# A decoder layer on one core: x ahead of w_ada, a new division of the start, and modulation loads spread

## The chip, the core and the metric

The kernel runs on one core of a Trainium2 chip. The metric is the device time of one execution, in microseconds (us), lower being better. A core has TensorE (PE: matmuls and transposes), VectorE (DVE), ScalarE (ACT), GpSimd (POOL) and SyncE (SP, which here issues nearly all transfers); each works through its own instructions in order, and semaphores make one wait for another.

## The reference, cut to what matters

One layer for 256 tokens of width 2048, all in float32. A vector `c` gives shift, scale and gate; the normed and modulated x goes through one input projection of 9296 columns; two kinds of attention, eight heads each, follow, and an output projection.

```
def _hybrid_layer(x, c, w_ada, b_ada, g_norm, w_in, ...):
    mod = jax.nn.silu(c) @ w_ada + b_ada
    shift, scale, gate = jnp.split(mod, 3, axis=-1)
    h = _rms_norm(x, g_norm) * (1.0 + scale[:, None, :]) + shift[:, None, :]
    proj = h @ w_in
    ...
    y = jnp.concatenate([ya, yb], axis=-1) @ w_out
    return x + gate[:, None, :] * y
```

`w_ada` is 2048 x 6144 (50 MB), `w_in` 2048 x 9296 (76 MB), `w_out` 2048 x 2048 (17 MB). All of the weights are read once.

## The kernel before, in words

**Matmuls.** Contraction runs over 16 k-tiles of 128 rows. `h` is kept transposed (k-tile by 256 tokens). Each float32 product is made of three matmuls in the fp32r type: a weight tile is cast to a high part `wh` (ScalarE, `cast_hi`, L306) and the rest `wl` (VectorE, `cast_lo`, L316), `h` likewise to `hhi` and `hlo`, and hi x hi, lo x hi and hi x lo are summed in PSUM (L760 to L762). For 512 columns, one k-tile and the two token tiles that is six matmuls. Column groups are named by what they hold (z, q, k, v, or the indexer's i0 to i2) and by a quad: `b0`, `b1`, `a0`, `a1`, so `qb0` is 512 columns of q.

**Passes.** The modulation of a k-tile needs two loads of `w_ada`, one for its shift and one for its scale, 128 columns by all 2048 rows each (1 MB, `gemv`, L273: a multiply and sum on VectorE against `s_row`, which holds silu(c)). It is made in chunks: k-tile 0, then 1, then two at a time. So the input projection goes over its column groups in passes, each taking the k-tiles whose modulation is known by then. The results of a pass leave PSUM in `evac`: the first of a group is copied (ScalarE, L662), later ones are added to it (VectorE, L664). A first pass with one k-tile takes a quad's four groups from one load (kind `quad`).

**What sets the order.** `loads` is a list written ahead by a planner that counts in `n_kt`, units of one k-tile by 512 columns: modulation loads come into it by `ADA_AT`, `ADA_FIRST` and `ADA_GAP`, in `between`. `issue` sends them from SyncE in this order into four `raw` buffers of 1 MB; a load waits until the buffer of the fourth load ahead of it has been cast or summed. `in_order` keeps a block's instructions in written order on each engine; elsewhere the framework's scheduler places them.

**The start.** The first part of `w_ada`, then x in eight tiles (token tile t, 512 columns j), then two halves of the second `w_ada` load with the first weights between them. ScalarE squares the x tiles (L339); VectorE (L342) and GpSimd (`rsqrt`, L135, L136) make `rx`, 1/rms of each token; x is scaled by it (L350, one tile on GpSimd, L348), transposed on TensorE into PSUM (`ptx`, L360) and copied out, times `g_norm`, as `xnT` (`x_gain`, L365). `build_h` makes `h` of a chunk from `xnT` and the modulation `mmod`. The transposes of later k-tiles and their copies stand among the matmuls of the first quads.

Of the kernel before, what the change touches and what calls it, by code (L numbers as in the profile page):

```python
# [35 lines left out]
# The modulation is made in chunks of k-tiles, shift and scale together; the input projection goes over its  # L36
# column groups in passes, each taking the k-tiles whose modulation is known by then.
# [12 lines left out]
def hybrid_block(ctx: ExitStack, tc: tile.TileContext, x, cols, w_ada_t, w_in, w_out, out):  # L50
# [24 lines left out]
    def in_order():  # L75
        # queues each of the block's instructions behind the one before it on its engine, over all such blocks
# [16 lines left out]
    # distance table: query tile 0 against keys 0..127, query tile 1 against keys 0..255  # L93
# [15 lines left out]
    # s = silu(c), and the products of the head gains with -1/sqrt(HD)  # L109
# [34 lines left out]
    # a load of w_ada: 128 of its columns, over all rows; h0, h1 bound the part of the rows  # L144
# [38 lines left out]
    while turn:  # L183
        while ready and (ready[0][0] <= n_kt or known == pos[turn[0]]):
# [38 lines left out]
    # the first weights come before the last part of the first chunk of the modulation  # L223
    n_start = 2 * CHUNKS[0][1] + 1
    loads.insert(n_start - 1, loads.pop(n_start))
    n_issued = 0
    late = []

    def issue(upto):
        nonlocal n_issued  # L230
        while n_issued < min(upto, len(loads)):
            ld = loads[n_issued]
            raw = rawp.tile([P, 2048], F32, tag="raw", name=f"raw{n_issued}")
            if ld["kind"] == "ada":
                h0, h1 = ld["h"]
                ld["v"] = raw[:, :h1 - h0]
                nc.sync.dma_start(ld["v"], w_ada_t[ld["col"] * P:(ld["col"] + 1) * P, h0:h1])
                while late:
                    nc.sync.dma_start(*late.pop(0))
            elif ld["kind"] == "quad":  # L240
                # the column groups of a quad are 1024 apart
# [562 lines left out]
```

## Time and profile before

| what | value |
|---|---|
| time, median of 3 runs | 578.87 us (578.55 to 581.14) |
| span of the profiled execution | 577.5 us |
| median of the runs over that span | 1.4 us |
| TensorE busy | 550.7 us, 95% |
| VectorE busy | 443.4 us, 77% |
| ScalarE busy | 325.4 us, 56% |
| GpSimd busy | 49.3 us, 9% |
| moved by DMA | 150.08 MB, 260 GB/s on average |

The profile shows one execution; its own time is not told apart from its span, so the median of the runs stands beside it. Busy shares are averages over stages with different limits: the first 50 us (x, the first modulation, two quads), the passes of the input projection until about 250 us, a stretch in which attention runs beside the last pass, and the output projection. In rows of the timeline a line is the start, the duration, the engine, the source line, the operation, what is written and read, and in brackets the idle time before it with what ended it. Neighbouring instructions of an engine overlap by about 0.1 us in such rows, so the step from start to start is the cost of one among many.

### The profile page before, as it was taken

To read this page: it belongs to the slowest core of one execution; us is meant where nothing else is said; L and a number is where in the kernel's file an instruction comes from. 1 tells how busy PE (TensorE), PEld (TensorE's weight loads), DVE (VectorE), ACT (ScalarE), POOL (GpSimd) and SP (SyncE) were. 2 spreads that over 40 slices of the span, in tenths; PEclk is the share of its full clock that TensorE was granted. 3 is DMA by queue.
4 is the path that set the end of the run, shared out by engine and by line. 5 is a ranking of instruction groups with operands and counts; after the bars stand their busy time and mean duration, and the time that the engine had idled before them with its cause. 6 is when DMAs were issued, how large, how long until landed. Compare 5 with 4: busy or idle time off the path is not lost.

```text
span 577.5 us, 7394 instructions
## 1 busy us (share of the span) xinstructions
PE 550.7 (95%) x2626; PEld 457.4 (79%) x2626; DVE 443.4 (77%) x675; ACT 325.4 (56%) x667; POOL 49.3 (9%) x61
## 2 busy tenths in 40 slices
PE   2869999999999999998999999999999999999996
PEld 2548888888878998976768888888877888887885
DVE  4876879898899797888979995788668576458452
ACT  5898563434435353567655567555766785554340
POOL 4100000000000000102101012010330210000000
PEclk8789999999999999999999999999999999999999
DMA  8988988989998898887864476777556468445701
GB/s 290 370 298 316 396 330 305 337 322 345 351 346 273 338 344 315 306 312 268 297 236 159 150 276 239 247 281 273 212 182 219 146 228 282 145 150 190 245 36 36
DMA packets 59669, 150.08 MB, mean 260 GB/s; under 512 B 3056, under 2 KB 9456, under 8 KB 53616
## 3 DMA queue, kind: packets, MB, share of 16 engines
q1 hardware_dynamic: 58480, 147.51, 71.4%
q10 hardware_dynamic: 1152, 2.10, 1.2%
q8 instruction: 20, 0.33, 0.2%
q14 instruction: 17, 0.14, 0.1%
HBM read 147.50 MB, written 2.10 MB: 259 GB/s over the span
## 4 chain that ended last, share of the span: by engine, by line
PE 80%; ACT 8%; DVE 4%; DMA 3%; POOL 2%; issue 2%; SPq 0%; DVEq 0%; ACTq 0%; POOLq 0%
PE mm_y_o L760 5%; PE mm_y_o L761 5%; PE mm_y_o L762 5%; PE mm_h_qa L760 2%; PE mm_h_ka L761 2%; PE mm_h_qa L762 2%; PE mm_h_qa L761 2%; PE mm_h_ka L762 2%; PE mm_h_ka L760 2%; PE mm_h_za L761 2%; PE mm_h_i L760 2%; PE mm_h_zb L762 2%; PE mm_h_zb L761 2%; PE mm_h_qb L760 2%; PE mm_h_qb L761 2%; PE mm_h_qb L762 2%
## 5 line engine op out<-in xcount | busy, mean ns | idle before, releaser
L306 ACT ACTIVATE wh<-raw 128x1024 fp32r<-128x1024 f32 (+3 forms) x192 | 187.1, 993 | 158.2 <-DMA raw<-in_w_in 60.6
L316 DVE TENSOR_TENSOR wl<-raw,wh 128x1024 fp32r<-128x1024 f32 (+3 forms) x192 | 215.2, 1140 | 61.9 <-ACT wh L306 61.4
L273 DVE CUSTOM_DVE_ANT_0 raw<-raw,s_row 128x2048 f32<-128x2048 f32 (+1 forms) x49 | 110.6, 2257 | 13.9 <-DMA raw<-in_w_ada_t 13.8
L760 PE MATMUL mm_y_o<-wh,yT 128*128 128x512 f32 x128 | 51.7, 404 | 0.0
L761 PE MATMUL mm_y_o<-wl,yT 128*128 128x512 f32 x128 | 49.9, 390 | 0.0
L762 PE MATMUL mm_y_o<-wh,yT 128*128 128x512 f32 x128 | 49.8, 390 | 0.0
L760 PE MATMUL mm_h_i<-wh,hhi 128*128 128x384 f32 (+1 forms) x96 | 31.5, 333 | 0.5 <-DVE p_i L664 0.5
L762 PE MATMUL mm_h_i<-wh,hlo 128*128 128x384 f32 (+1 forms) x96 | 31.5, 329 | 0.0
L761 PE MATMUL mm_h_i<-wl,hhi 128*128 128x384 f32 (+1 forms) x96 | 31.5, 328 | 0.0
L760 PE MATMUL mm_h_za<-wh,hhi 128*128 128x512 f32 x64 | 26.3, 413 | 4.6 <-ACT wh L306 4.6
L762 PEld LDWEIGHTS mm_y_o<-wh,yT 128*128 128x128 f32 x128 | 24.0, 188 | 5.3 <-DVE yT L554 0.2
L760 PEld LDWEIGHTS mm_y_o<-wh,yT 128*128 128x128 f32 x128 | 24.1, 188 | 4.8 <-ACT yT L553 0.2
L761 PEld LDWEIGHTS mm_y_o<-wl,yT 128*128 128x128 f32 x128 | 24.1, 188 | 4.6
L760 PE MATMUL mm_h_kb<-wh,hhi 128*128 128x512 f32 x64 | 26.0, 406 | 0.2 <-ACT p_zb L662 0.2
L760 PE MATMUL mm_h_vb<-wh,hhi 128*128 128x512 f32 x64 | 25.7, 403 | 0.2 <-ACT p_qb L662 0.2
L760 PE MATMUL mm_h_zb<-wh,hhi 128*128 128x512 f32 x64 | 25.9, 408 | 0.0
L761 PE MATMUL mm_h_za<-wl,hhi 128*128 128x512 f32 x64 | 25.7, 402 | 0.1
L760 PE MATMUL mm_h_qb<-wh,hhi 128*128 128x512 f32 x64 | 25.7, 401 | 0.0
L760 PE MATMUL mm_h_qa<-wh,hhi 128*128 128x512 f32 x64 | 25.7, 409 | 0.0
L760 PE MATMUL mm_h_ka<-wh,hhi 128*128 128x512 f32 x64 | 25.4, 402 | 0.0
L762 PE MATMUL mm_h_za<-wh,hlo 128*128 128x512 f32 x64 | 25.3, 398 | 0.0
L760 PE MATMUL mm_h_va<-wh,hhi 128*128 128x512 f32 x64 | 25.2, 397 | 0.0
(215 smaller groups left out, 1208.4 us busy)
## 6 DMA issues: line engine op xcount, KB each, us to landing
raw<-in_w_in SPq DMA_DIRECT2D x51, 1024.0 KB, 6.0
raw<-in_w_ada_t SPq DMA_DIRECT2D x47, 1024.0 KB, 6.7
raw<-in_w_out SPq DMA_DIRECT2D x16, 1024.0 KB, 5.1
raw<-in_w_in SPq DMA_DIRECT2D x17, 512.0 KB, 4.5
raw<-in_w_in SPq DMA_DIRECT2D x11, 768.0 KB, 6.2
x<-in_x SPq DMA_DIRECT2D x8, 256.0 KB, 6.9
xr<-in_x ACTq DMA_DIRECT2D x8, 256.0 KB, 6.5
raw<-in_w_in SPq DMA_DIRECT2D x3, 672.0 KB, 5.5
```

The lines of the kernel that those rows point to most:

```text
L273: nc.vector.tensor_tensor_reduce(out=ld["v"], in0=ld["v"], in1=s_row[:, h0:h1], scale=1.0, scalar=0.0, op0=ALU.mult, op1=ALU.add, accum_ou ...
L306: nc.scalar.activation(hi[:, :n, :w], v, AF.Copy)
L316: nc.vector.tensor_tensor(lo[:, :n, :w], v, sb["hi"][:, :n, :w].bitcast(F32), op=ALU.subtract)
L760: nc.tensor.matmul(ps, a_hi, sb["hi"][:, i, :w], start=st, stop=False)
L761: nc.tensor.matmul(ps, a_hi, sb["lo"][:, i, :w], start=False, stop=False)
L762: nc.tensor.matmul(ps, a_lo, sb["hi"][:, i, :w], start=False, stop=en)
```

## The change

What it does, in the order of the program:

- x's eight tiles are issued first; then the two first `w_ada` loads, whole, in five pieces (1024, 1024 | 1024, 512, 512 rows), each piece with a sum of its own (`PARTS`); then the first quad's `q` group, its other three groups, and the second quad. Until then the second quad stood behind four loads of modulations.
- The loads of modulations that follow come at `ADA_NEXT`, then each 5.5 units as before.
- The eight squares are made by ScalarE (six) and VectorE (two); of the scales by `rx`, five are on ScalarE and three on GpSimd. All 32 transposes of x stand ahead of the first matmul. The result for k=8 to 15 is copied to SBUF; k=0 too; k=1 to 7 stay in PSUM until `build_h` reads them there.
- `g_norm` is no longer multiplied into `xnT`, but into the modulation's scale (`build_h`, and `start_mod` on GpSimd for k-tile 0).
- A quad's groups are cast two at a time, in the order q, k, v, z (for the first quad q alone, k with v, z alone); of a quad's evacuations, those of the second token tile of a pair's second group are on VectorE.
- `build_gate` waits for two steps between its addition and its transposes.

```diff
-ADA_AT, ADA_FIRST, ADA_GAP, ADA_LAG, GATE_AT, GATE_GAP = 4, 4, 5.5, 2, 150, 8
+ADA_NEXT, ADA_GAP, ADA_LAG, GATE_AT, GATE_GAP = (8, 8, 11, 14, 17, 20), 5.5, 2, 150, 8
+PARTS = ((0, 1024, 2048), (0, 1024, 1536, 2048))
...
+    for ld, parts in zip(loads, PARTS):
+        ld["parts"] = list(zip(parts, parts[1:]))
...
+    ada_at = list(ADA_NEXT)
+    ada_at += [ADA_NEXT[-1] + ADA_GAP * (i + 1) for i in range(len(ada) - len(ada_at))]
...
-        if ada and n_kt >= ada_at:
-            for _ in range(ADA_FIRST if ada_at == ADA_AT else 1):
-                ld = ada.pop(0)
...
+        if ada and n_kt >= ada_at[0]:
+            ada_at.pop(0)
+            ld = ada.pop(0)
+            loads.append(ld)
+            if "end" in ld:
+                ready.append((n_kt + (ADA_LAG if ld["end"] > 1 else 0), CHUNKS[ld["end"]][1]))
...
+            first = len(loads) == len(PARTS)
+            for lo, hi in ((0, 1), (1, 3), (3, 4)) if first else ((0, 2), (2, 4)):
+                for i in range(lo, hi):
+                    members[i]["pair"] = (lo, hi)
...
+            if (kind, c, o) == ("mod", 0, 3):
+                start_mod()
...
+        sb["i"] = ld.get("i", 0)
+        if sb["i"]:
+            sb["hi"] = subs[j - 1]["hi"]
+            return
...
     def start_mod():
...
-        nc.vector.tensor_tensor(ss[:, :m], ss[:, :m], bmod[:, :m], op=ALU.add)
+        nc.gpsimd.tensor_scalar(ss[:, 5:6], ss[:, 0:1], ss[:, 1:2], bmod[:, 0:1], op0=ALU.add, op1=ALU.add)
+        nc.gpsimd.tensor_scalar(ss[:, 6:7], ss[:, 2:3], ss[:, 3:4], bmod[:, 1:2], op0=ALU.add, op1=ALU.add)
+        nc.gpsimd.tensor_scalar(ss[:, 6:7], ss[:, 6:7], gcol[:, 0:1], 0.0, op0=ALU.mult, op1=ALU.add)
...
         if b == 0:
...
+            nc.vector.scalar_tensor_tensor(ss[:, 6:7], ss[:, 4:5], gcol[:, 0:1], ss[:, 6:7],
+                                           op0=ALU.mult, op1=ALU.add)
+            ss = ss[:, 5:7]
+            cast_lo(0)
         else:
             nc.vector.tensor_tensor(ss[:, :2 * n], ss[:, :2 * n], bmod[:, 2 * k0:2 * k1], op=ALU.add)
+            nc.vector.tensor_tensor(ss[:, n:2 * n], ss[:, n:2 * n], gcol[:, k0:k1], op=ALU.mult)
...
+            src = xnT[k]
+            if 0 < k < 8:
+                src, xnT[k] = ptx[k // 2][:, k % 2 * L:(k % 2 + 1) * L], h_tile(f"xnT{k}")
...
+    with in_order():
+        for i in range(6):
+            x_square(i, "act")
+            if i == 3:
+                x_rsqrt(0)
+        for i in range(6, 8):
+            x_square(i, "dve")
+        x_rsqrt(1)
+        for t, j, eng in ((0, 0, "act"), (0, 2, "act"), (0, 1, "pool"), (0, 3, "act"),
+                          (1, 0, "act"), (1, 2, "pool"), (1, 3, "act"), (1, 1, "pool")):
+            x_scale(t, j, eng)
+        for t in range(2):
+            for j in (0, 2, 3, 1):
+                x_transpose(t, j)
+        for k in (0, 8, 9, 10, 11):
+            x_copy(k)
+    with in_order():
+        for i in range(n_start):
+            gemv(loads[i])
+        next_load = n_start
+        cast_hi(0)
+        for _ in build_h(0):
+            pass
+        for k in range(12, 16):
+            x_copy(k)
...
+                    if "pair" in ld and t == 1 and ld["i"] == 1:
+                        nc.vector.tensor_copy(proj[g, t][:, :w], ps[:, :w])
```

What stands in the program's order, at three places. The first is the start of SyncE's transfers, behind `cc`. Before:

```order
L237 DMA raw_148<-in_w_ada_t 128x2048
L331 DMA x_0_150<-in_x 128x512
...
L331 DMA x_3_164<-in_x 128x512
L237 DMA raw_171<-in_w_ada_t 128x1024
L249 DMA raw_173<-in_w_in 128x512
L237 DMA raw_175<-in_w_ada_t 128x1024
L239 DMA raw_173<-in_w_in 128x3x512
L237 DMA raw_209<-in_w_ada_t 128x2048
L237 DMA raw_212<-in_w_ada_t 128x2048
L237 DMA raw_214<-in_w_ada_t 128x2048
L237 DMA raw_315<-in_w_ada_t 128x2048
L253 DMA raw_317<-in_w_in 128x4x512
```

and now (of x's eight tiles the first and the last stand here, in both):

```order
L342 DMA x_0_148<-in_x 128x512
...
L342 DMA x_3_162<-in_x 128x512
L244 DMA raw_164<-in_w_ada_t 128x1024 x2
L244 DMA raw_167<-in_w_ada_t 128x1024
L244 DMA raw_167<-in_w_ada_t 128x512 x2
L252 DMA raw_171<-in_w_in 128x512
L252 DMA raw_171<-in_w_in 128x3x512
L252 DMA raw_268<-in_w_in 128x4x512
L244 DMA raw_270<-in_w_ada_t 128x2048
L244 DMA raw_272<-in_w_ada_t 128x2048
L260 DMA raw_325<-in_w_in 128x2x512
L260 DMA raw_383<-in_w_in 128x2x512
```

The second quad (`raw_317`, now `raw_268`) has moved from behind four loads of modulations to ahead of them, and only two come before the first weights of two k-tiles.

The second place is VectorE at the second quad. Before (`raw_315` is a load of modulations, `raw_317` the quad):

```order
L397 TENSOR_TENSOR hlo_351<-xnT_251,hhi_348 128x256
L273 ISA raw_315,mmod_328<-raw_315,s_row 128x2048
L273 ISA mmod_328 128x1
L316 TENSOR_TENSOR wl_333<-raw_317,wh_331 128x512
L316 TENSOR_TENSOR wl_366<-raw_317,wh_364 128x512
L316 TENSOR_TENSOR wl_393<-raw_317,wh_391 128x512
L316 TENSOR_TENSOR wl_409<-raw_317,wh_407 128x512
```

and now:

```order
L328 TENSOR_TENSOR wl_329<-raw_268,wh_327 128x1024
L680 COPY p_vb_1_341<-mm_h_vb_1_332 128x512
L274 ISA raw_270,mmod_389<-raw_270,s_row 128x2048
L274 ISA mmod_389 128x1
L328 TENSOR_TENSOR wl_357<-raw_268,wh_355 128x1024
L680 COPY p_ka_1_381<-mm_h_ka_1_372 128x512
L274 ISA raw_272,mmod_389<-raw_272,s_row 128x2048
```

The quad's four low parts are two, and a sum of a modulation load now stands between them.

The third place is TensorE behind the quads, where the first groups of two k-tiles begin. Before (`wh_425` is the only load's cast that it needs there):

```order
L760 MATMUL mm_h_za_0_468<-wh_425,hhi_242 128x512
L760 MATMUL mm_h_za_1_469<-wh_425,hhi_242 128x512
L761 MATMUL mm_h_za_0_468<-wl_427,hhi_242 128x512
L762 MATMUL mm_h_za_0_468<-wh_425,hlo_245 128x512
L760 MATMUL mm_h_za_0_468<-wh_425,hhi_348 128x512
```

and now (`wh_392` is cast from `raw_325`, `wh_418` from `raw_383`):

```order
L775 MATMUL mm_h_za_0_444<-wh_392,hhi_279 128x512
L775 MATMUL mm_h_za_1_445<-wh_392,hhi_279 128x512
L775 MATMUL mm_h_qa_0_471<-wh_418,hhi_279 128x512
L776 MATMUL mm_h_za_0_444<-wl_394,hhi_279 128x512
L777 MATMUL mm_h_za_0_444<-wh_392,hlo_283 128x512
L776 MATMUL mm_h_za_1_445<-wl_394,hhi_279 128x512
```

A matmul of the next group, on the next load's cast, has moved ahead of the first group's low parts.

## Rows read from the trace of the kernel before

**Rows 1.** The page: busy us of an engine, share of the span, instructions.
```profile
PE 550.7 (95%) x2626; PEld 457.4 (79%) x2626; DVE 443.4 (77%) x675; ACT 325.4 (56%) x667; POOL 49.3 (9%) x61
```

**Rows 2.** Stages: length, busy us of each engine, granted clock, DMA share, GB/s.
```profile
0.00:20.50 20.50, 7.61 (x32) 6.12 (x33) 10.71 (x23) 11.14 (x26) 8.91 (x29) 0.76 0.90 326
20.50:34.50 14.00, 9.01 (x42) 6.31 (x41) 11.45 (x14) 14.00 (x33) 0.00 (x0) 0.98 0.97 353
34.50:50.00 15.50, 15.37 (x59) 11.95 (x60) 11.13 (x11) 12.75 (x21) 0.00 (x0) 0.89 0.83 271
...
50.00:250.00 200.00, 199.40 (x953) 172.13 (x952) 172.91 (x200) 97.23 (x138) 1.61 (x2) 1.00 0.91 332
```

**Rows 3.** Waits of TensorE, the second longest: total us, times, longest.
```profile
PE mm_h_za L760 <- ACT wh L306: 4.6, 1, 4.6
```

**Rows 4.** Timeline: the issue of x's tiles, and the first and last square.
```profile
1.63 4.85 SPq L331 DMA_DIRECT2D x<-in_x  x8
...
8.00 0.63 ACT L339 ACTIVATE junkx<-x 128x512 f32<-128x512 f32 x1 [5.12 <-DMA x<-in_x]
...
13.03 0.63 ACT L339 ACTIVATE junkx<-x 128x512 f32<-128x512 f32 x1
```

**Rows 5.** Timeline: GpSimd and VectorE beside each other at the start.
```profile
11.60 0.58 POOL L136 TENSOR_TENSOR rx<-rx,mhalf 128x1 f32<-128x1 f32 x1
...
14.27 1.23 DVE L273 CUSTOM_DVE_ANT_0 raw<-raw,s_row 128x1024 f32<-128x1024 f32 x1 [0.33 <-DMA raw<-in_w_ada_t]
14.30 1.62 POOL L136 TENSOR_TENSOR rx<-rx,mhalf 128x1 f32<-128x1 f32 x1
...
16.02 0.83 POOL L348 TENSOR_SCALAR x<-x,rx 128x512 f32<-128x512 f32 x1
16.21 0.15 DVE L373 TENSOR_TENSOR mmod<-mmod,cc 128x1 f32<-128x1 f32 x1
16.28 1.64 DVE L273 CUSTOM_DVE_ANT_0 raw<-raw,s_row 128x1024 f32<-128x1024 f32 x1
```

**Rows 6.** Timeline of TensorE: first transposes and matmul, two slow steps, two full ones.
```profile
3.45 3.65 PE L119 MATMUL pts<-ident,s_col 128*128 128x128 f32 x16 [3.45 <-DVE s_col L114]
...
20.57 0.72 PE L760 MATMUL mm_h_zb<-wh,hhi 128*128 128x512 f32 x1
...
36.29 0.63 PE L760 MATMUL mm_h_za<-wh,hhi 128*128 128x512 f32 x1
36.71 0.63 PE L761 MATMUL mm_h_za<-wl,hhi 128*128 128x512 f32 x1
...
41.74 0.39 PE L762 MATMUL mm_h_va<-wh,hlo 128*128 128x512 f32 x1
41.97 0.84 PE L760 MATMUL mm_h_za<-wh,hhi 128*128 128x512 f32 x2
```

**Rows 7.** Timeline of ScalarE between 24 and 39 us.
```profile
24.28 1.07 ACT L662 ACTIVATE p_zb<-mm_h_zb 128x512 f32<-128x512 f32 x2
...
31.56 2.41 ACT L365 ACTIVATE xnT<-ptx,cc 128x256 f32<-128x256 f32 x6
33.70 2.35 ACT L306 ACTIVATE wh<-raw 128x512 fp32r<-128x512 f32 x4
...
38.30 1.06 ACT L306 ACTIVATE wh<-raw 128x1024 fp32r<-128x1024 f32 x1
```

**Rows 8.** Transfers issued at 37.05 and 27.35 us: KB each, us to landing.
```profile
raw<-in_w_in SPq DMA_DIRECT2D x1, 512.0 KB, 4.3
raw<-in_w_in SPq DMA_DIRECT2D x1, 1024.0 KB, 5.3
```

**Rows 9.** VectorE by shape, 45 to 250 us: count, busy us, mean ns, idle before.
```profile
L316 DVE TENSOR_TENSOR wl<-raw,wh 128x1024 fp32r<-128x1024 f32 x54 | 64.3, 1220 | 11.5 <-ACT wh L306 11.5
L273 DVE CUSTOM_DVE_ANT_0 raw<-raw,s_row 128x2048 f32<-128x2048 f32 x27 | 61.7, 2284 | 2.6 <-DMA raw<-in_w_ada_t 2.6
...
L664 DVE TENSOR_TENSOR p_za<-mm_h_za,p_za 128x512 f32<-128x512 f32 x4 | 2.8, 688 | 1.3 <-PE mm_h_za L762 1.3
```

More of the change, by code (lines that the diff above doesn't have):

```diff
@@ L183, in hybrid_block @@
     while turn:
+        while ada and (n_kt >= ada_at[0] or (known == pos[turn[0]] and not ready)):
+            ada_at[0] = min(n_kt, ada_at[0])
+            between()
         while ready and (ready[0][0] <= n_kt or known == pos[turn[0]]):
@@ L221, in hybrid_block @@
                                 q == QUADS[-1], True, True))
[L224 to L225 removed]
+    n_start = 2 * CHUNKS[0][1]
     n_issued = 0
[L227 removed]
     def issue(upto):
@@ L234, in issue @@
             if ld["kind"] == "ada":
[L235 to L239, printed above, removed]
+                ld["v"] = raw
+                for h0, h1 in ld.get("parts", [(0, D)]):
+                    nc.sync.dma_start(raw[:, h0:h1], w_ada_t[ld["col"] * P:(ld["col"] + 1) * P, h0:h1])
             elif ld["kind"] == "quad":
@@ L332, in hybrid_block @@
             xt.append(xx)
+    issue(n_start + 1)
     ssx = consts.tile([P, 8], F32, name="ssx")
     rx = consts.tile([P, 2], F32, name="rx")
-    def x_norm(t):
-        for j in range(4):
-            junk = work.tile([P, 512], F32, name=f"junkx{t}{j}", tag="big", bufs=2)
-            with in_order():
-                nc.scalar.activation(junk, xt[4 * t + j], AF.Square, accum_out=ssx[:, 4 * t + j:4 * t + j + 1])
-        r = rx[:, t:t + 1]
-        with in_order():
-            nc.vector.tensor_reduce(r, ssx[:, 4 * t:4 * t + 4], axis=mybir.AxisListType.X, op=ALU.add)
-            rsqrt(r, r, D)
@@ L363, in x_gain, with x_square, x_rsqrt @@
-    def x_gain(k):
+    def x_square(i, eng):
+        junk = work.tile([P, 512], F32, name=f"junkx{i}", tag="big", bufs=2)
+        if eng == "act":
+            nc.scalar.activation(junk, xt[i], AF.Square, accum_out=ssx[:, i:i + 1])
+        else:
+            nc.vector.tensor_tensor_reduce(out=junk, in0=xt[i], in1=xt[i], scale=1.0, scalar=0.0, op0=ALU.mult,
+                                           op1=ALU.add, accum_out=ssx[:, i:i + 1])
+    def x_rsqrt(t):
+        nc.vector.tensor_reduce(rx[:, t:t + 1], ssx[:, 4 * t:4 * t + 4], axis=mybir.AxisListType.X, op=ALU.add)
+        rsqrt(rx[:, t:t + 1], rx[:, t:t + 1], D)
@@ new lines, in hybrid_block, with x_scale, x_transpose @@
+    xnT, ptx = {}, {}
+    def x_scale(t, j, eng):
+        xx = xt[4 * t + j]
+        if eng == "act":
+            nc.scalar.activation(xx, xx, AF.Copy, scale=rx[:, t:t + 1])
+        else:
+            nc.gpsimd.tensor_scalar(xx, xx, rx[:, t:t + 1], 0.0, op0=ALU.mult, op1=ALU.add)
+    def x_transpose(t, j):
+        for k in range(4 * j, 4 * j + 4):
+            k2, i = k // 2, k % 2
+            if k2 not in ptx:
+                ptx[k2] = ps_tile(("tr", "s", "pt", "pv")[k2], f"ptx{k2}") if k2 < 4 else mm_tile(f"ptx{k2}")
+            nc.tensor.transpose(ptx[k2][:, i * L + t * P:i * L + (t + 1) * P],
+                                xt[4 * t + j][:, (k % 4) * P:(k % 4 + 1) * P], ident)
@@ L644, in hybrid_block @@
             cast_lo(j)
-        for k in range(CHUNKS[0][1], 4):
-            x_gain(k)
-        x_scale(2)
-        x_scale(3)
     acc_ps = {}
@@ L712, in hybrid_block @@
         ld = sb["ld"]
-        if 1 <= j <= 4:
-            with in_order():
-                x_transpose(3 + j)
-                for k in range(3 * j + 1, 3 * j + 4):
-                    x_gain(k)
         if ld["kset"] == "h":
```

114 lines of the change are left out of this document (34 added, 80 removed).

## The prediction

> **What bounds the kernel now.** I read the table of stages first, then the list of waits, then the timeline of the start. TensorE is busy for 550.7 of 577.5 us [rows 1], and by stages [rows 2] it is busy for 199.4 of the 200 us from 50 to 250, at a granted clock of 1.00: there it is the bound, and nothing on another engine is worth anything unless TensorE has to wait for it. The reader should see how different the first 50 us are: 7.6 of 20.5 us busy before the first matmul, 9.0 of 14.0 us behind it. Of its waits the longest behind the first matmul is 4.6 us for the cast `wh` of the second quad [rows 3]. The first matmul starts at 20.57 and the 48 matmuls of the two quads are through at 41.97 [rows 6], when the first group of two k-tiles begins. At the full rate a 512-column matmul steps 0.23 us [rows 6], so 48 of them are 10.9 us of work, and 21.4 were spent (24 transposes are in there as well). So the change can win what lies before 41.97, and the question is what it pays behind it. Since the number of matmuls is the same, I follow one quantity: when a given count of them is done.
>
> **The first matmul.** Before, x lands between 8.0 and 13.0: the squares, which wait for it, start then [rows 4]. With nothing but `cc` ahead, its first tile is issued at about 1.2 instead of 1.63 and does not queue behind 1 MB of `w_ada`. In the trace the first x tile lands 6.4 us after its issue and the others follow at 5.0/7 = 0.72 us each. Bounds for the last tile: 8.1 (first one in 2.4 us after its issue, the rest at 0.65) and 9.7 (the first one slow again). I take 9.7, since a slow first tile is what the trace shows. Behind it `w_ada` and the first weights land at the same pace, at about 11.0, 12.3, 13.6, 14.2, 14.9 (the five pieces) and 15.5; the other three groups at 17.5, the second quad at 20.1.
>
> The price of the new division of labour is in VectorE and GpSimd, which hold each other up [rows 5]: `pow` on one column takes 0.58 us alone and 1.62 beside a w_ada sum, and that sum takes 1.64 instead of 1.23 beside a GpSimd scale of 0.83. GpSimd now has three such scales and three small operations of `start_mod`, all beside the five sums. VectorE ends the last square at 10.5 and the reduce at 10.7; `pow` is held by the first sum until 12.7; then scales and sums take turns: a scale ends 0.56 after the sum that holds it (14.05, 15.75, 16.8), and a sum behind a scale takes 0.42 more (pieces end at 13.5, 15.2, 16.25, 17.3). `start_mod` ends at 17.95 and the modulation at 18.25. Beside it TensorE transposes at 0.21 each, the step at the lower clock level [rows 6]; tiles j=2 are through at 16.65, ScalarE copies k=8 to 11 at 0.36 each (18.1), casts the first group (0.52 [rows 7], 18.65) and writes `hhi` (19.15). First matmul at **19.2, a gain of 1.4**. Bounds: 17.0, if x comes early and nobody is held, and 20.5, if the transposes alone, all behind the last scale, end the wait.
>
> **The two quads.** What ScalarE did from 20.6 to 34.5 was seven scales and copies of k-tiles among the casts and evacuations, and the second quad had been issued only at 27.35, behind four loads of modulations. Now the quad's load stands before them. ScalarE between `hhi` and the cast of the quad's last pair: four copies (1.45), casts 0.95, 0.52, 0.95, 0.95, six evacuations of 0.48 less one that VectorE takes (2.4 left, [rows 7]): 7.2, until 26.3. VectorE then does the sum of `raw_270`, which stands ahead of `wl_357` (the second place of the order above), from 25.7 to 27.95, and the low part until 29.15; nine matmuls are left, so the 48 end at **31.3: 12.1 instead of 21.4, a gain of 9.3**. The copies moved to VectorE and the paired casts cost nothing here, because VectorE waits for ScalarE in this stretch; the seven copies that are left out (2.5 us) are part of the sum.
>
> **What comes back behind it.** Here the loads are the thing to follow. There are four raw buffers. The second weight load of two k-tiles (`raw_383`) takes the quad's buffer, which is free when `wl_357` ends, at 29.2. A 512 KB load that has the queue to itself lands 4.3 us after its issue [rows 8]: 33.5. Its cast (0.95) and the evacuation behind it (0.48) end at 34.95, and TensorE's order (third place) has `qa_0` on that cast third, ahead of the ready low parts. So TensorE does two matmuls and stands from 31.8 to 34.95: **3.15 lost**. That stall is set by 29.15 + 4.3 + 1.4, whenever the quads end. From there the loads of chunk 2 of the modulation lie between the weights at every third unit instead of 5.5. Following buffer, issue, 4.3 to 5.5 us of landing [rows 8], cast, sum or low part (2.28 and 1.22 less 0.08 of overlap [rows 9]) for the next ten loads, I get TensorE short of a low part by 0.5 at `va`, 0.5 at `i0`, 1.2 at `zb` and 0.6 at `qb`, and 0.1 at `ka`: **2.9 lost**; the 72nd matmul is done at 40.0 instead of 47.7, `qb` of the last quad at 62.4. From then on the modulation comes at the old pace. Eight more additions of partial sums on VectorE (0.69 each) lie in the 200 us where it is busy for 172.9 [rows 2], so I count them at nothing; without that slack they would cost 5.5. The seven products of the modulation with `g_norm` are new, 0.15 each by a sum of the same size [rows 5], and hidden in the same slack. That k=1 to 7 stay in PSUM takes four banks that only the background work of the last pass and the gates use: nothing. The later `build_gate` transposes have no wait of TensorE to remove in rows 3: nothing. From 250 on I take the stalls as they are.
>
> Sum: 577.5 - 1.4 - 9.3 + 3.15 + 2.9 = 572.85 of span. The median of the runs is 578.87, 1.4 over the span shown, and I keep that: **574.2 us**. A measurement of this kernel tells about 0.5% from no change, 2.9 us.
>
> **A rule against the change.** Rows 4 show 256 KB tiles, once queued, landing every 0.72 us, and rows 8 a lone 512 KB load taking 4.3, of which 1.4 is that pace and 2.9 is what a transfer pays when nothing hides it. The Trainium skill, DMA: Bandwidth & Descriptors, section Bandwidth, wants transfers of at least 1 MiB for three quarters of the peak; the change cuts two such loads into five. The trace does not bear that out for queued transfers, so the sum goes by the rows. By the rule the case "pieces pay" below would be the result.
>
> **Rivals.**
> - *Nothing is held and the small stalls hide* (0.17). First matmul at 17.0 and only the 3.15 behind the quads: 574.2 - 2.2 - 2.9 = 569.1. For it: 8.1 would follow if the late first tile of x belonged to the load ahead of it. Against: the holding in rows 5 is in the very instructions that the change multiplies.
> - *The clock falls in the new stall* (0.20). Before, TensorE stood for 4.6 us until 34.54, and the next seven matmuls stepped 0.43 and more instead of 0.23 [rows 3, 6]; the stretch from 34.5 to 50 has a mean clock of 0.89 [rows 2]. The new stall is 3.15. Falling there costs 7 x 0.2 = 1.4; a second time, behind one of the short ones, 2.8: 575.6 to 577.0.
> - *Loads come too slowly: slower* (0.10). My schedule has 14 loads from `raw_383` on at 1.8 us each. Each 0.1 us more a load is 1.4 us; at 2.34 the gain is gone and 2.9 more, so it is slower by 0.5%; at 2.5 it gives 584. Before, from 34 to 58 us, loads were issued some 2.2 us apart, but TensorE was full then and asked for no more.
> - *Pieces pay* (0.05). Two more transfers at 2.9 each ahead of the first matmul: 580.0.
>
> **How the numbers follow.** The forecast has 0.48, with a range of its own of 572 to 576 (half of the bounds of the first matmul, and 1 us either way in the small stalls). The range reaches to the first rival below and past the clock's case above, 569.0 to 579.0; it leaves out the slow loads, the pieces and a little below 569, under 2 in 10. Faster by over 0.5% is below 576.0: the forecast, the first rival and a small part of the clock's case less the forecast's own tail, 0.66. Slower by over 0.5% (above 581.8) is the slow loads, 0.10. Within: 0.24.
>
> **What would show it.** Right: the first matmul at 18.5 to 20; GpSimd scales of 0.8 to 1.5 us and w_ada pieces of 1.6; the second quad's matmuls over by 31 to 32; one wait of TensorE of about 3 us for `wh` of the second two-k-tile load; short waits for `wl` or `wh` until 62; nothing new from 62 to 250. Wrong: squares that begin at 3.6 and pieces of 1.23 (first rival); a granted clock of 0.5 at 35 (second); several waits over 2 us for `raw` between 38 and 62 (third), above all if TensorE waits there for w_in or w_ada landings longer than 5.5 us after their issue. It would also be wrong if VectorE, fuller by 5.5 us, made TensorE wait between 62 and 250.

## The result, and the profile after

The changed kernel takes 584.79 us (median of 5 runs, 584.23 to 585.1) against 578.75 of the kernel before in the same runs: a ratio of 1.0098, 95% interval 1.0075 to 1.0122. It is 1% slower. The profiled execution has a span of 583.0, against 577.5.

The busy times of the page, to be laid beside [rows 1]:

```profile
PE 554.7 (95%) x2626; PEld 458.2 (79%) x2626; DVE 451.8 (77%) x698; ACT 318.6 (55%) x648; POOL 49.3 (8%) x66
```

The table of stages, with the stages of [rows 2] first and three shorter ones behind them (columns: length, busy time of each engine, granted clock, DMA share, GB/s):

```profile
0.00:20.50 20.50, 10.44 (x46) 9.27 (x47) 11.04 (x26) 10.46 (x25) 13.57 (x34) 1.00 0.90 313
20.50:34.50 14.00, 13.13 (x54) 9.48 (x52) 12.00 (x15) 13.19 (x24) 0.11 (x1) 1.00 0.70 252
34.50:50.00 15.50, 13.02 (x54) 9.46 (x55) 11.85 (x14) 9.08 (x16) 0.00 (x0) 1.00 0.93 328
50.00:250.00 200.00, 195.81 (x893) 164.12 (x892) 174.67 (x202) 93.03 (x122) 0.00 (x0) 0.99 0.93 330
24.00:28.00 4.00, 4.00 (x18) 2.93 (x17) 3.47 (x5) 4.00 (x8) 0.00 (x0) 1.00 0.57 191
28.00:32.00 4.00, 4.00 (x19) 3.34 (x18) 4.00 (x5) 3.94 (x7) 0.00 (x0) 1.00 0.38 100
32.00:70.00 38.00, 31.69 (x131) 23.66 (x129) 27.70 (x32) 23.48 (x39) 0.00 (x0) 0.96 0.96 351
```

From 20.5 to 34.5 TensorE is busy for 13.1 us instead of 9.0: the stage that the change is about does what it should. But while it works there, the DMA stands for half of the time (shares 0.57 and 0.38), and from 32 to 70 the DMA is full and TensorE has 6.3 us of waits. There are nine of them, and the three longest are these (in total, times, longest):

```profile
PE mm_h_zb L775 <- ACT wh L315: 1.5, 1, 1.5
PE mm_h_qa L775 <- ACT p_za L682: 1.1, 1, 1.1
PE mm_h_za L777 <- DVE hlo L424: 0.9, 1, 0.9
```

To see where time is won and lost I follow one quantity, as the prediction does: the time at which a given number of the projections' matmuls (each weighted by its step at the full rate) has begun, in one trace less the same in the trace of before. Minus is ahead. Between 250 and 500 us the attention's matmuls lie in another order among them, so there only the end counts.

| kernel | at 31 | 55 | 80 | 115 | 245 | at the end |
|---|---|---|---|---|---|---|
| changed | -8.3 | -3.2 | +2.3 | +2.3 | +2.4 | +5.1 |
| e_scales_act | -8.7 | -5.0 | +0.5 | +0.5 | +0.4 | +3.2 |
| e_gate170 | -8.4 | -2.8 | +2.5 | +2.5 | +2.6 | -0.7 |
| e_raw5 | -9.2 | -5.7 | -1.8 | -1.8 | -1.9 | (attention altered) |
| e_four_behind | -8.9 | -1.6 | -0.3 | +0.4 | +0.7 | +4.3 |
| e_old_order | | +1.7 | +1.6 | +3.0 | +3.8 | +2.7 |
| e_before_spread | -4.0 (at 36) | -1.6 | +4.0 | +4.0 | +3.7 | +7.7 |
| e_combo3 | -8.4 | -4.5 | -0.6 | -0.6 | +0.2 | -3.0 |

So the changed kernel is 8.3 us ahead at 31, has given back 10.6 by 80, keeps its place to 245, and loses 2.7 more behind that. Each line is one profiled execution, so differences of a microsecond between two kernels can be chance.

**The start.** GpSimd from 13 us on (line, operation, tile, count, idle time before):

```profile
13.28 1.57 POOL L139 TENSOR_TENSOR rx<-rx,mhalf 128x1 f32<-128x1 f32 x1
14.85 4.69 POOL L368 TENSOR_SCALAR x<-x,rx 128x512 f32<-128x512 f32 x3
19.53 0.38 POOL L392 TENSOR_SCALAR mmod<-mmod,cc 128x1 f32<-128x1 f32 x1
```

and TensorE's first matmul:

```profile
21.61 0.50 PE L775 MATMUL mm_h_qb<-wh,hhi 128*128 128x512 f32 x1 [0.30 <-ACT hhi L417]
```

The three scales take 4.69 us instead of 3 x 0.83, since VectorE's sums lie beside them [rows 5], and `start_mod` queues behind them. The last tile of x landed at 11.9.

**Behind the quads.** VectorE has no gap from 26 to 37 us:

```profile
26.08 1.23 DVE L328 TENSOR_TENSOR wl<-raw,wh 128x1024 fp32r<-128x1024 f32 x1 [0.26 <-ACT wh L315]
27.22 0.68 DVE L680 COPY p_vb<-mm_h_vb 128x512 f32<-128x512 f32 x1
27.82 2.28 DVE L274 CUSTOM_DVE_ANT_0 raw<-raw,s_row 128x2048 f32<-128x2048 f32 x1
30.03 1.22 DVE L328 TENSOR_TENSOR wl<-raw,wh 128x1024 fp32r<-128x1024 f32 x1
31.17 0.69 DVE L680 COPY p_ka<-mm_h_ka 128x512 f32<-128x512 f32 x1
31.77 2.28 DVE L274 CUSTOM_DVE_ANT_0 raw<-raw,s_row 128x2048 f32<-128x2048 f32 x1
```

The two modulation loads landed at 25.0 and 27.4 and are summed at 27.8 and 31.8; until then and until the low parts are made their buffers are held, and SyncE can issue only two loads between 19.4 and 31 (at 25.85 and 30.14). That is why the DMA stands. The quads' 48 matmuls are through at 33.66; TensorE does two matmuls more and then stands until 35.42:

```profile
33.66 0.61 PE L775 MATMUL mm_h_za<-wh,hhi 128*128 128x512 f32 x2
35.42 0.50 PE L775 MATMUL mm_h_qa<-wh,hhi 128*128 128x512 f32 x1 [1.15 <-ACT p_za L682]
```

**Late.** TensorE's waits from 245 to 360 us (in total, times, longest):

```profile
PE mm_h_i L775 <- DVE p_i L684: 2.0, 2, 1.4
PE pgate L435 <- DVE ygb L578: 1.5, 1, 1.5
PE lg L481 <- ACT qi L475: 1.1, 1, 1.1
PE mm_h_i L775 <- DVE p_qb L684: 0.8, 1, 0.8
```

In the kernel before this stretch has a wait of 1.4 for `lg`, one of 1.1 for `ptq` and none of `mm_h_i`. The first of them, on VectorE and then on TensorE:

```profile
248.34 2.28 DVE L274 CUSTOM_DVE_ANT_0 raw<-raw,s_row 128x2048 f32<-128x2048 f32 x1
...
250.55 1.28 DVE L684 TENSOR_TENSOR p_qb<-mm_h_qb,p_qb 128x512 f32<-128x512 f32 x2
```

```profile
250.21 0.39 PE L777 MATMUL mm_h_qb<-wh,hlo 128*128 128x512 f32 x1
251.38 0.39 PE L775 MATMUL mm_h_i<-wh,hhi 128*128 128x336 f32 x1 [0.78 <-DVE p_qb L684]
```

A load of the gate is being summed when the group `qb` ends; its evacuation has to stand behind the sum, and the next group's first matmul waits for it. (With the gate's loads later, in run 6 below, the first of the two evacuations starts at 249.68 instead of 250.55.) The longest, 1.37 us, ends at 266.30. It leads back to a small GpSimd step beside the next gate's sum (258.00 to 260.28), for which ScalarE waits 2.8 us. Here are the two, and below them the same step in run 6, where no sum lies beside it:

```profile
258.48 1.86 POOL L138 TENSOR_SCALAR sm<-sm 128x2 f32<-128x2 f32 x1 [237.86 <-ACT junki L452]
266.30 0.41 PE L775 MATMUL mm_h_i<-wh,hhi 128*128 128x384 f32 x1 [1.37 <-DVE p_i L684]
```

```profile
257.90 0.48 POOL L138 TENSOR_SCALAR sm<-sm 128x2 f32<-128x2 f32 x1 [238.34 <-ACT junki L452]
```

### The profile page after: what moved, and what is told of

It reads as the page before. It is cut to its first block, busy times and chain, and to the rows that moved or that the text cites. A ratio compares the mean times of both kernels' runs of the same rounds, so it can differ in the third digit from the quotient of the medians.

```text
span 583.0 us, 7393 instructions
## 1 busy us (share of the span) xinstructions
PE 554.7 (95%) x2626; PEld 458.2 (79%) x2626; DVE 451.8 (77%) x698; ACT 318.6 (55%) x648; POOL 49.3 (8%) x66
## 4 chain that ended last, share of the span: by engine, by line
PE 70%; DVE 12%; ACT 7%; DMA 5%; issue 3%; POOL 2%; SPq 0%; DVEq 0%; ACTq 0%
PE mm_y_o L775 5%; PE mm_y_o L777 5%; PE mm_y_o L776 5%; DVE wl L328 5%; DVE raw L274 3%; DMA raw<-in_w_in 3%; ACT wh L315 3%; PE mm_h_i L775 2%; PE mm_h_ka L775 2%; PE mm_h_va L777 2%; PE mm_h_va L776 2%; PE mm_h_qa L777 2%; PE mm_h_ka L777 2%; PE mm_h_ka L776 2%; PE mm_h_i L776 2%
## 5 line engine op out<-in xcount | busy, mean ns | idle before, releaser
L274 DVE CUSTOM_DVE_ANT_0 raw<-raw,s_row 128x2048 f32<-128x2048 f32 (+2 forms) x51 | 110.9, 2177 | 8.4 <-DMA raw<-in_w_ada_t 8.3
L776 PE MATMUL mm_h_zb<-wl,hhi 128*128 128x512 f32 x64 | 25.9, 404 | 0.7 <-DVE wl L328 0.7
L777 PE MATMUL mm_h_zb<-wh,hlo 128*128 128x512 f32 x64 | 25.7, 401 | 0.0
L776 PE MATMUL mm_h_kb<-wl,hhi 128*128 128x512 f32 x64 | 25.2, 393 | 0.5 <-DVE wl L328 0.5
```

Source lines behind the costliest of these rows:

```text
L274: nc.vector.tensor_tensor_reduce(out=ld["v"][:, h0:h1], in0=ld["v"][:, h0:h1], in1=s_row[:, h0:h1], scale=1.0, scalar=0.0, op0=ALU.mult, o ...
L776: nc.tensor.matmul(ps, a_hi, sb["lo"][:, sb["i"] + i, :w], start=False, stop=False)
L777: nc.tensor.matmul(ps, a_lo, sb["hi"][:, sb["i"] + i, :w], start=False, stop=en)
```

## The experiments

Theory S: the order of loads behind the quads starves TensorE until 73 us. Rival W: the new start costs the time. Rival L: it is lost late. Each run is compared with runs of the kernel before on the same chip.

**1. e_old_order**, the modulations where the kernel before has them:

```diff
-ADA_NEXT, ... = (8, 8, 11, 14, 17, 20), ...
+ADA_NEXT, ... = (4, 4, 4, 4, 9.5, 15), ...
```

> The changed kernel with the modulation loads at 4, 4, 4, 4, 9.5, 15 units, where the kernel before had them, and everything else of the change kept. Theory S (the spread order starves TensorE from 34 to 73 us, since too few weights come in and buffers are held; of 8.3 us won it gives back 10.6): TensorE waits once, behind the first 24 matmuls, for some 8 us, and then no more before 120; at 120 it has lost no more than 1.5 us against the kernel before, and the time is 579 to 581. Rival L (the loss is made late, behind 340 us, by the kinds of segments and the gate's wait): 583 to 586, with 3 to 5 us lost behind 340. Rival W (the new start itself costs it): the first matmul still at 21.6, 1.0 later than before, which gives at most 580.

582.05 us, 1.0051 (1.0032 to 1.0071), above the 579 to 581 of S and below the 583 to 586 of L. One wait of 6.1 us for `wh` of `za`, then nothing as long; but it is 1.7 us behind already at 55. It loses nothing behind 245 (+3.8, then +2.7), where the changed kernel loses 2.7. So the late loss goes with the order of loads, and L and S are both right in part.

**2. e_four_behind**, four modulation loads right behind both quads:

```diff
-ADA_NEXT, ... = (8, 8, 11, 14, 17, 20), ...
+ADA_NEXT, ... = (8, 8, 8, 8, 13.5, 19), ...
```

> The changed kernel with modulation loads at 8, 8, 8, 8, 13.5, 19 units: both quads first, then the four loads that the kernel before had ahead of the second quad. Theory S: TensorE waits once, from 33 us on, for 8 to 10 us (4 MB at 2.6 us each) instead of in eight small stalls; then the modulation is ahead and no wait for wh or wl follows before 70; at 120 us it stands within 1.5 us of the kernel before: 578 to 581. Rival L: 583 to 586. If VectorE's full stretch from 21 to 37 us is what holds the buffers, the four sums (2.28 us each) make that stall longer than 10 us, and the time is over 582.

586.24 us, 1.0123 (1.0096 to 1.0151). Ahead of 120 it did what S expects (one wait of 4.9 us, within 0.4 of the kernel before at 115, 1.9 better than the changed kernel), but 3.6 us were lost behind 245. L is as large as S.

**3. e_before_spread**, the kernel before with the change's planner alone (its constants stand here; the planner's lines that read them are changed with them):

```diff
-ADA_AT, ADA_FIRST, ADA_GAP, ADA_LAG, GATE_AT, GATE_GAP = 4, 4, 5.5, 2, 150, 8
+ADA_NEXT, ADA_GAP, ADA_LAG, GATE_AT, GATE_GAP = (8, 8, 11, 14, 17, 20), 5.5, 2, 150, 8
...
```

> The kernel before with the new order of loads alone (modulations at 8, 8, 11, 14, 17, 20 units, then each 5.5): old start, old casts, g_norm in the copies. Theory S: what the second quad wins is given back until 73 us, and the time is 582 to 586, slower than before. Rival W (the start of the change is what costs): 575 to 579, not slower. Rival L, if the late loss comes from the segments, which the order makes: also 582 to 586, but with the loss behind 340 us and a lag under 1 us at 120.

586.89 us, 1.0125 (1.0096 to 1.0153): both losses are there with the old start, +4.0 at 80 and 4.0 more behind 245. The order makes them, and W is not the main cause.

**4. e_raw5**, five raw buffers:

```diff
-rawp ... bufs=4
+rawp ... bufs=5
-            issue(next_load + 4)
+            issue(next_load + 5)
-... qk bufs=2, nb bufs=2, pT bufs=2, at bufs=4
+... qk bufs=1, nb bufs=1, pT bufs=1, at bufs=3
```

> The changed kernel with five raw buffers and issue one load further ahead; to make room, the attention's tiles qk, nb, pT have one buffer instead of two and at three instead of four, so only what lies ahead of 250 us is read from it. Theory S in the form that buffers held by VectorE leave the DMA idle from 24 to 32 us: the idle DMA stretch is filled by another load, TensorE's waits between 34 and 68 us shrink from about 8.5 us to 4 or less, and at 120 us the kernel is 3 to 5 us ahead of the changed one. If instead it is the order of loads alone (more bytes wanted than the DMA carries): waits of 7 to 9 us as before, at most 1.5 us ahead at 120.

583.73 us, 1.0082 (1.0053 to 1.0111); at 115 us it is 4.1 us ahead of the changed kernel (the attention's tiles were cut as well, so its time tells nothing). Three stages, to be laid beside those above:

```profile
24.00:28.00 4.00, 4.00 (x18) 3.29 (x18) 3.54 (x4) 4.00 (x8) 0.00 (x0) 1.00 0.99 376
28.00:32.00 4.00, 4.00 (x19) 3.33 (x18) 4.00 (x5) 3.65 (x8) 0.00 (x0) 1.00 0.46 130
32.00:70.00 38.00, 33.51 (x145) 25.01 (x144) 30.73 (x35) 24.63 (x40) 0.00 (x0) 1.00 0.99 369
```

The first is filled now. From 31 to 115 it gives back 7.4 us instead of 10.6; the other 0.9 of the 4.1 it has won ahead of 31. So held buffers are at most 3.2 of the 10.6: in this execution the clock did not fall either, which cost the changed kernel 1.4 at 59 to 62 us, and the two are not told apart. The loads themselves came no faster: the 14 behind `raw_383` landed from 29.2 to 62.5, 2.38 us each, against 2.36 in the changed kernel. The fifth buffer starts them earlier; their pace is the DMA's, which is full.

**5. e_scales_act**, the start's GpSimd scales on ScalarE:

```diff
-        for t, j, eng in ((0, 0, "act"), (0, 2, "act"), (0, 1, "pool"), (0, 3, "act"),
-                          (1, 0, "act"), (1, 2, "pool"), (1, 3, "act"), (1, 1, "pool")):
+        for t, j, eng in ((0, 0, "act"), (0, 2, "act"), (0, 1, "act"), (0, 3, "act"),
+                          (1, 0, "act"), (1, 2, "act"), (1, 3, "act"), (1, 1, "act")):
```

> The changed kernel with the three scales of x on GpSimd given to ScalarE, nothing else. Theory W2 (the late first matmul comes from GpSimd: its three scales are stretched to 4.69 us by VectorE's sums and hold start_mod until 20.6): the first matmul at 19.3 to 20.0 instead of 21.6, sums of w_ada at 1.23 throughout, start_mod done by 18.5. If theory S holds (behind the quads the loads set the pace, not the start), a part of that is lost again at the wait for the third load of weights, and the time is 582.5 to 584.5. Rival (x's landing sets the start): first matmul 21 or later, no change of the time.

583.2 us, 1.0081 (1.0049 to 1.0112). First matmul at 19.50, the sums of 1024 rows 1.22 to 1.23 each, and 1.9 us are won in the profiled execution. The ratios, 1.0081 against 1.0098, do not tell this from nothing. GpSimd in it:

```profile
12.79 1.52 POOL L139 TENSOR_TENSOR rx<-rx,mhalf 128x1 f32<-128x1 f32 x1
15.29 2.50 POOL L392 TENSOR_SCALAR mmod<-mmod,cc 128x1 f32<-128x1 f32 x1 [0.98 <-DVE mmod L274]
```

Little of it is the start: 2.1 us are won at the first matmul, and 0.3 are left when the quads are through, at 33.34. The granted clock was 0.5 until 23.6 in this execution, and the first nine matmuls stepped 0.43 instead of 0.23, which costs 2.0:

```profile
20.10 0.63 PE L776 MATMUL mm_h_qb<-wl,hhi 128*128 128x512 f32 x1
20.52 0.63 PE L775 MATMUL mm_h_qb<-wh,hhi 128*128 128x512 f32 x1
```

The rest comes behind the quads. With this edit the scheduler also sums the first modulation at 24.5, ahead of the second quad's low parts (27.8 above), the next weights are issued at 26.8 instead of 30.1, and the wait of 1.1 at `qa` is gone. e_gate170 shows the same of an early start: its execution happened to reach the first matmul at 20.56, 1.05 earlier than the changed kernel, the first matmuls stepped 0.43 there too, and the quads are through at 33.54.

**6. e_gate170**, one number:

```diff
-... GATE_AT, GATE_GAP = ... 150, 8
+... GATE_AT, GATE_GAP = ... 170, 8
```

> The changed kernel with the first load of the gate after 170 units instead of 150, so that no gate sum stands between the narrow groups i2, i0 and i1 of the last pass. Theory G (the late part of the loss is VectorE's gate sums of 2.28 us standing ahead of the evacuations of groups that last about 2 us): the three waits of mm_h_i at 250, 257 and 265 us (2.75 us together) are gone, nothing changes ahead of 240, and the time is 581 to 582.5, the lower end if the wait of pgate at 350 (1.5 us) goes too. Rival (VectorE is simply too full from 240 to 360): other waits of 2 to 3 us take their place, 584 to 585.5.

579.05 us, 1.0011 (0.999 to 1.0032), span 577.2: 5.8 us of span, 5.0 by the ratios, more than expected, and the changed kernel is level with the one before. Up to 245 the lag differs by 0.4 at most. Of TensorE's waits behind 245, 6 us in all in the changed kernel, two are left:

```profile
PE mm_h_i L775 <- DVE p_i L684: 0.6, 1, 0.6
PE pgate L435 <- DVE ygb L578: 0.5, 1, 0.5
```

**7. e_copies**, the quads' three copies on VectorE given back to ScalarE:

```diff
-                    if "pair" in ld and t == 1 and ld["i"] == 1:
+                    if False:
                         nc.vector.tensor_copy(proj[g, t][:, :w], ps[:, :w])
```

> The changed kernel with the quads' evacuations all on ScalarE, so VectorE has three copies (0.69 each) less between 27 and 37 us. Theory S in the form that VectorE's full stretch holds the raw buffers: the loads behind the quads are issued 0.6 to 2 us earlier, TensorE's waits from 33 to 68 us are 1 to 2 us shorter, and the time is 583 to 584. Rival (ScalarE's casts and evacuations hold the quads): the 48 matmuls end at 34 or later instead of 33.2, and the time is 585 or more. Rival (the order of loads alone): no difference.

585.05 us, 1.0116 (1.0095 to 1.0137): no difference. It is about 1 us ahead of the changed kernel from 35.5 to 41 and 0.1 at 52; waits of 1.6 (`va`) and 1.8 (`zb`) for `wh` took it. Counting these copies at nothing was right.

**8. e_combo1**, 5 and 6 together and three quads for k-tile 0:

```diff
-ADA_NEXT, ... GATE_AT, ... = (8, 8, 11, 14, 17, 20), ... 150, ...
+ADA_NEXT, ... GATE_AT, ... = (12, 12, 12, 12, 17.5, 23), ... 170, ...
```

> The changed kernel with three changes: the scales of x all on ScalarE, the gate's loads from 170 units on, and modulation loads at 12, 12, 12, 12, 17.5, 23 units, so that three quads are loaded for k-tile 0 and four modulations come together behind them. By the theories together: first matmul at 19.7; 72 matmuls on k-tile 0 (16.3 us) cover the four modulations, TensorE waits less than 4 us between 33 and 70 and is 2 to 4 us ahead of the kernel before at 120; no waits of mm_h_i at 250 to 266: 574 to 578, faster than before by 0.2 to 0.8%. If VectorE's sums and low parts hold the buffers whatever the order, one wait of 6 us or more comes at 36 to 45 and the time is 579 to 582.

587.5 us, 1.0168 (1.0125 to 1.021), a miss. It was 4.3 us ahead at 45 and 4.1 behind at 117: eight waits of 0.4 to 1.2 us, most for `wh` or `wl`, lie between 39 and 82, the granted clock was 0.5 from 42.1 to 49.0, and over five more us went behind 245, with a wait of 3.0 at 438. The planner makes the later passes anew with these numbers; what in them costs most was not taken apart.

**9. e_combo3**, the edits of 5 and 6 together, and **10. e_combo2**, those and the edit of 2.

> The changed kernel with two edits: the scales of x all on ScalarE and the gate's loads from 170 units on; the spread order of the modulations is kept. If both add up: a span of 583.0 - 1.9 - 5.8 = 575.3, a time of 576.5 to 577.5, not told apart from the kernel before or just faster; the lag at 120 us then is +0.5 as in the run of the scales alone, so the whole loss is two places, the start and the gate, and the spread order by itself is worth nothing. If not additive: 579 or more.

> The changed kernel with three edits that were run alone before: the scales of x all on ScalarE (1.9 us in the run of it), the gate's loads from 170 units on (5.8 us) and the four modulation loads of the old order together behind both quads (2.6 us at 120 us in the run of it). If the three places are independent, as the ledger of theories S, W2 and G has it, the span is 583.0 - 1.9 - 5.8 - 2.6 = 572.7 and the time 574 to 575, faster than before by 0.6 to 0.9%. If the clock falls in the long wait behind the quads, or the start's gain is lost in it, 576 to 578.

e_combo3: 576.18 us, 0.9944 (0.9924 to 0.9964), span 574.9, faster than the kernel before. 583.0 - 1.9 - 5.8 = 575.3 was expected, and in spans the two add up. By the ratios they win 8.9 us on the changed kernel together and 6.0 as a sum, at the edge of what the intervals allow; in this execution the clock did not fall at 59. e_combo2: 577.12, 0.9958 (0.9938 to 0.9978), span 574.4 instead of 572.7: four modulations together take 0.5 off the span and nothing off the median, so the gain of run 2 does not add to the others.

**11. e_ada_first**, the first 1 MB of `w_ada` ahead of x again:

```diff
+    issue(1)
     xt = []
     for t in range(2):
```

> The changed kernel with the first load of w_ada (1 MB, in its two pieces) ahead of x again, as the kernel before has it, the rest of the change kept. The prediction put x ahead at about 1 us of an earlier x. If x's landing sets the start: x lands about 2 us later, the first matmul at 23 to 24 instead of 21.6, the time 586 to 587. If GpSimd's scales and the w_ada sums set it: two sums are then out of the way when the scales run, the first matmul at 21 to 22.3, the time 584 to 585.5.

587.36 us, 1.0134 (1.0107 to 1.0161), span 584.0. The first matmul is at 23.62, 2.0 later, and 1.0 of it is left at the end. In this execution the clock did not fall at 59 to 62, where the changed kernel lost 1.4, and by the ratios the difference is 2.1 us, with intervals that overlap. So x ahead is worth 1 to 2 us.

**12. e_before_gate170**, the kernel before with the edit of 6:

```diff
-ADA_AT, ADA_FIRST, ADA_GAP, ADA_LAG, GATE_AT, GATE_GAP = 4, 4, 5.5, 2, 150, 8
+ADA_AT, ADA_FIRST, ADA_GAP, ADA_LAG, GATE_AT, GATE_GAP = 4, 4, 5.5, 2, 170, 8
```

> The kernel before with the gate's loads from 170 units on, nothing else. It tells whether 150 was a bad place in itself or only with the new order. Theory G, by place: the trace of before has no wait of mm_h_i behind 245 us, and its waits there (1.45, 1.09, 0.49, 0.37) are of the attention's own: the time within 1.5 us of before, 577 to 580. Rival (gates so early cost VectorE time in any order): faster by 2 us or more, 576 or less.

591.32 us, 1.0198 (1.0171 to 1.0226): 12 us slower, against both expectations. TensorE's longest waits behind 245:

```profile
PE lg L453 <- ACT qi L447: 4.2, 2, 3.3
PE pgate L407 <- DVE yga L550: 3.2, 1, 3.2
PE ptq L445 <- ACT qkb L513: 1.8, 1, 1.8
```

Behind the first, ScalarE waits 6.0 us for GpSimd's `ssqb`. GpSimd and VectorE there:

```profile
262.29 5.36 POOL L135 TENSOR_SCALAR ssqb<-ssqb 128x8 f32<-128x8 f32 x1 [17.30 <-ACT jqb L485]
267.73 1.65 POOL L136 TENSOR_TENSOR ssqb<-ssqb,mhalf 128x8 f32<-128x8 f32 x1
```

```profile
261.89 3.48 DVE L316 TENSOR_TENSOR wl<-raw,wh 128x1024 fp32r<-128x1024 f32 x3
265.30 2.28 DVE L273 CUSTOM_DVE_ANT_0 raw<-raw,s_row 128x2048 f32<-128x2048 f32 x1
267.51 0.08 DVE L273 DVE_READ_ACCUMULATOR2_ANT mgate<- 128x1 f32 x1
```

A scale of eight columns, 0.20 us elsewhere in the same trace (at 353.5 us, for one), lasts 5.36, until VectorE has done three low parts and a gate sum without a pause. Behind each of TensorE's two waits of 3 us and more the granted clock is 0.5 for 3.4 us. The slow matmuls there, 15 at some 0.2 us more each, cost 3.3 of the 11 us that are lost behind 245.

**13. e_gate162** (the changed kernel, `GATE_AT` 162) and **14. e_before_gate158** (the kernel before, `GATE_AT` 158), to tell a bad neighbour from gates that come too late.

> The changed kernel with the gate's loads from 162 units on: the first then falls between the two loads of i0, the second behind i1; none stands where the run at 150 has its sums at 248.3 and 258.0 us. Theory G in its closer form (a gate sum does harm where an evacuation or GpSimd's power for the indexer stands behind it): the waits of mm_h_i at 251 and 266 us go, at most one other wait of up to 1.5 us comes, and the time is 579 to 581. Rival (any gate among the narrow groups costs the same): 583 or more.

> The kernel before with the gate's loads from 158 units on, a place between 150 and the 170 that cost it 12 us: the first gate behind i1. If the time depends on what stands beside the attention's first steps and not on early or late as such: anywhere from 577 to 591, with each microsecond over the kernel before found as a wait of TensorE between 250 and 500 us for an attention step of ScalarE or GpSimd. If lateness of the gates as such is what costs: about a third of the 12 us, 582 to 584.

e_gate162: 585.44 us, 1.0102 (1.0072 to 1.0132), not the 579 to 581 expected. The two long waits of `mm_h_i` are gone; in their place:

```profile
PE sb L547 <- ACT rl L484: 3.0, 1, 3.0
```

at 322 us, where ScalarE had waited 4.6 us for this:

```profile
316.31 3.48 POOL L138 TENSOR_SCALAR ssqb<-ssqb 128x8 f32<-128x8 f32 x1 [12.24 <-ACT jqb L513]
```

e_before_gate158: 590.45 us, 1.018 (1.0123 to 1.0238). GpSimd's first `ssqb` takes 5.33 us, ScalarE waits 6.0 and TensorE 3.3 for `lg`, as at 170. So 8 units later cost the old order as much as 20: it is not lateness as such. In all three runs the longest wait leads back to a small GpSimd step that a gate's sum stands beside. The other waits of e_before_gate158 (4.5 us for `pgate`, 1.1 for `ptk`) were not followed, and slow matmuls cost 3.3 there too.

## Why the prediction was wrong, step by step

The span came out 10.15 us above the forecast's 572.85. Three terms of the sum make 9.65 of it: the first matmul (2.4 late), the stalls behind the quads (10.6 instead of 6.05), and the stalls from 250 on, counted as unchanged (2.7).

**First matmul at 19.2.** It came at 21.61 (20.56 to 21.61 in the profiles of the seven kernels with this start). The last tile of x landed at 11.9, not 9.7, and this is 2.2 of the 2.4: the first six came 0.64 to 0.89 apart, but the seventh 2.4 behind the sixth, and `w_ada` moved in that gap. Behind it the working held step for step: each of GpSimd's scales ended about 0.5 behind a VectorE sum, as worked out, only the second was held through two of them (2.17 us), so the three took 4.69 instead of 4.1; what follows was 0.3 shorter. x ahead does pay, 1 to 2 us (run 11). Without the GpSimd scales the first matmul comes 2.1 earlier (run 5), 0.5 of it by an x that landed earlier in that execution.

**The two quads over at 31.3.** They took 12.05 us (21.61 to 33.66) against 12.1 in the sum. The number is right, but that it would have held with a first matmul at 19.2 is not shown. They took 13.8 us from 19.50 in run 5 (clock at 0.5, then a wait of 0.6 for a low part) and 13.8 from 19.74 in run 9 (at the full clock, with a wait of 1.5 for a low part behind a modulation's sum).

**A stall at `qa_0` until 34.95.** It ended at 35.42. Right in place, but the number is two errors against each other: `raw_383` did not wait for the quad's low part, which ended at 31.25, but was issued at 30.14, when the sum of the first modulation was over; that is 0.9 later than worked out, and it landed in 3.6 us instead of 4.3. Since the quads ended later, the stall is 1.15 long and not 3.15.

**Small stalls of 2.9 and loads at 1.8 us each.** This is the step that failed most. The 14 loads behind `raw_383` landed from 33.7 to 66.8, 2.36 us each; 2.34 was the point of the rival "loads come too slowly", to which I gave 0.10. They are 11.1 MB, so 1.8 us each would have been 440 GB/s. The DMA moved 353 at a share of 0.97 [rows 2], 351 at 0.96 here and 369 at 0.99 in run 4, and over short stretches at most 425 (20.5 to 24 us); at 369 the 14 loads take 30 us (an estimate from these numbers), 4.9 more than my schedule had. I followed each load's buffer and landing and never added up their bytes. The landings were too short as well: I took 4.3 to 5.5 us, which rows 8 show for transfers with the queue nearly to themselves; with the queue full, loads of 1 MB landed 6.7 to 8.4 us behind their issue. The page of before had it:

```profile
raw<-in_w_ada_t SPq DMA_DIRECT2D x47, 1024.0 KB, 6.7
```

And I had the first modulation's sum at 25.7, the next loads soon behind it; the sums ran at 27.8 and 31.8, and the DMA lost 0.43 x 4 + 0.62 x 4 = 4.2 us ahead of a stretch in which it could not catch up. TensorE lost 10.6 instead of 6.05: about 6.4 in nine waits, 1.4 to 1.6 in slow matmuls at the clock of 0.5, the rest in the steps behind each wait. No single wait is over 1.5, so the sign that I had named for this rival, several waits over 2 us, did not come. Five buffers save at most 3.2 of it (run 4); another order stands 1.9 better at 115 (run 2), of which 0.8 is left at the end.

**The clock.** It fell to 0.5 from 59.1 to 62.5, behind waits of 1.5 and 0.5 us, not in the stall at 34:

```profile
60.00:64.00 4.00, 4.00 (x13) 3.15 (x13) 3.62 (x3) 2.50 (x4) 0.00 (x0) 0.69 1.04 399
```

That is the rival's price, 1.4, in another place. The forecast had no term for it.

**The rule against the change** (the Trainium skill, DMA: Bandwidth & Descriptors, section Bandwidth). The pieces landed at 13.2, 14.5, 15.8, 16.4 and 17.1: 1.29 for 512 KB and 0.67 for 256 KB, the pace of whole loads (2.5 for 1 MB). Queued pieces cost nothing; the trace disagrees with the rule here.

**"From 250 on I take the stalls as they are."** It counted at nothing a place that the change moves, and 2.7 us were lost there. `GATE_AT` stands in the same units as before, but the order of loads, the passes and the attention's steps around it are others. One number is worth 5 to 5.8 us in the changed kernel (run 6), more than was lost: with it, 3.3 us are won on the kernel before behind 245. The cause is shown for single waits: a gate sum ahead of an evacuation (at 250), and GpSimd's small steps held through VectorE's sums and low parts, with ScalarE and then TensorE behind them (at 258, and runs 12 to 14). Why 150 suits the old order and 170 the new I can only read off afterwards; no rule for a good place was tested.

Eight more additions on VectorE and the copies: nothing, as predicted (from 80 to 245 the changed kernel's lag moves by 0.1; run 7).

## What to carry to other kernels

Add up the bytes of a schedule of loads and compare them with what the DMA moves when it is full, before following buffers and landings one by one. A load that is moved ahead moves everything that is placed by count behind it: look again at each number that places other work, to the end of the program. When a stage is made faster, ask which buffers it hands back and when; if the DMA stands meanwhile, that time returns as waits later. Keep GpSimd's small steps out of stretches in which VectorE works without a pause on two SBUF inputs, above all where ScalarE waits for them.

## What the runs showed of the hardware

A small GpSimd step can be held through several VectorE instructions that follow each other: 5.36, 5.33 and 3.48 us for a scale of eight columns that takes 0.20 (runs 12, 14 and 13), and 2.50 for one of one column that takes 0.38 (run 5). It is not always the whole row: the changed kernel's scales of 512 columns got in between two sums. VectorE's sums beside it stay at 1.22 when GpSimd does only such steps (run 5), and grow to 1.57 beside its scales of 512 columns. The Trainium skill, SBUF — State Buffer, section Who interferes with whom, says that a VectorE instruction with two SBUF inputs contends with a GpSimd instruction that reads SBUF; the trace agrees, and shows the wait to run over several such instructions in a row.
